# Layer norm of a convolution mixer: small products pinned in TensorE's order, its steps with priority, ACT's tables loaded early, the first four output chunks together, a tap every 2.9 blocks

## The chip, the core and the metric

The kernel runs on one core of a Trainium2 chip. The time is the device time in microseconds from launch to end; lower is better. PE is TensorE (matmuls; PEld its weight loads), DVE is VectorE, ACT is ScalarE, POOL is GpSimd, SP is SyncE, whose queue issues the weight transfers.

## The reference

Two layers at 256 tokens of 2048 features in float32. Layer 0 mixes with a convolution branch and a pooling branch, layer 1 with a short convolution; each is followed by a gated feed-forward block of 5632. The change lies in layer 0's mixer:

```python
def conv_pool_mixer(x, norm_g, w_in, conv_w, conv_b, ln_g, ln_b, w_pool, pool_scale, w_out):
    h = rms_norm(x, norm_g)
    u = h @ w_in
    a_val = u[..., :D_CONV]
    a_gate = u[..., D_CONV:2 * D_CONV]
    b_in = u[..., 2 * D_CONV:]
    a = a_val * jax.nn.sigmoid(a_gate)
    a = causal_depthwise_conv(a, conv_w) + conv_b
    a = jax.nn.silu(layer_norm(a, ln_g, ln_b))
    p = multiscale_pool(b_in, w_pool, pool_scale)
    return jnp.concatenate([a, p], axis=-1) @ w_out
```

D_CONV is 1024 and the convolution has 31 taps. The layer norm runs over those 1024 features of a token.

## The kernel before

Features lie on the 128 partitions in chunks of 128, tokens (256) along the free axis. A weight block is 128 x 128. Weights arrive on SP's queue in an order fixed by `_layout`, and are split on the core in pieces of eight blocks into a rounded part `hi` (a cast on ACT, L125) and a rest `lo` (a subtraction on DVE or, for the blocks in `POOL_SPLIT`, on POOL, L132). `hi` and `lo` have six buffers each, and a piece is prepared four pieces ahead. In the mixer a block's product is three matmuls (L177 to L179): `hi` by the rounded half of the input, `hi` by its rest, `lo` by the rounded half. The accumulators `acc` have five banks; the small totals `st` share one bank.

The mixer runs in this order: input projections of the convolution and pooling chunks (`M0_ORDER`); the small products of the pooling branch, which write `xs` anew through `split` (L210 on ACT, L211 on DVE); the pool half of the output projection, `project(xs, POOL_CHUNKS)`, 16 output chunks of eight blocks, each added to the residual `h` (L324); then the convolution half, `project(cat, range(NA), norm)`, 16 chunks of eight blocks.

Beside this the convolution runs on DVE and ACT. `tick` is called after each block's product and takes steps from queues by the costs in `PACE`: a tap of two chunks every 3.2 blocks (`tap`, L397 on ACT, L400 to L404 on DVE), into the tile `side`. Behind the third of the four pairs the mean of six chunks is taken (`ln_mean`, L431) and subtracted (`ln_center`). Behind the fourth pair (`convolved`, L410) come `ln_shift` (the rest of the mean, L457 and L450), `ln_squares` (the variance, L450), `ln_rstd` (`spread_over`: root, reciprocal and one refining step, then a diagonal `diag` that the product L274 spreads over all partitions) and `ln_out` (scale, Silu, split into `cat`: L481 to L486). `drain` empties the queues ahead of the convolution half. ACT needs a table for Sqrt, one for Sigmoid and one for Silu, and loads it where the function first occurs after another.

What is written in this order is then placed by a scheduler with priorities, which fixes each engine's order of instructions; every engine issues in that order.

Of the kernel before, what the change touches and what calls it, by code (L numbers as in the profile page):

```python
# [11 lines left out]
F32 = mybir.dt.float32  # L12
# [5 lines left out]
P = 128  # L18
# [66 lines left out]

WARM = 9

POOL_SPLIT = range(96, 24 * NC + 16 + 7 * NC + 8)
# [3 lines left out]
PACE = {"dve": 3.2, "ln": 3.0, "wait": 1.0, "now": 0.0}  # L92
# [3 lines left out]
def block_kernel(ctx: ExitStack, tc: tile.TileContext, xtok: bass.AP, vec: bass.AP, wall: bass.AP, out: bass.AP):  # L96
# [55 lines left out]
    queues = {name: deque() for name in ("dve", "ln", "wait")}  # L152
# [19 lines left out]
    def product(acc, hi, lo, x, first, last, wide):  # L172
        if wide:
            nc.tensor.matmul(acc, hi, x, start=first, stop=False, skip_group_check=True)  # L174
            nc.tensor.matmul(acc[:, T:], lo, x[:, :T], start=False, stop=last, skip_group_check=True)  # L175
        else:
            nc.tensor.matmul(acc[:, :T], hi, x[:, :T], start=first, stop=False)  # L177
            nc.tensor.matmul(acc[:, :T], hi, x[:, T:], start=False, stop=False)  # L178
            nc.tensor.matmul(acc[:, :T], lo, x[:, :T], start=False, stop=last)  # L179
# [43 lines left out]
    nc.gpsimd.memset(ones, 1.0)  # L223

# [14 lines left out]
    def rsqrt_of(*totals, scale, halves=False, st=None):  # L239
# [9 lines left out]
        return spread_over(small, st, scale, halves)  # L249

    def spread_over(small, st, scale, halves=False):
# [3 lines left out]
        nc.scalar.activation(root, st, AF.Sqrt, scale=scale, bias=eps)  # L255
        nc.vector.tensor_scalar(out=var, in0=st, scalar1=scale, scalar2=EPS, op0=ALU.mult, op1=ALU.add)
# [7 lines left out]
        spread = [ps.tile([P, P], F32, name="half", tag="acc") for _ in range(2)] if halves else None  # L264
        for j in range(2):
            nc.vector.tensor_tensor(out=diag[:, j * P : (j + 1) * P], in0=identity, in1=e[:, j : j + 1].broadcast_to([P, P]), op=ALU.mult)
            if halves:
                nc.tensor.matmul(spread[j], ones, diag[:, j * P : (j + 1) * P], start=True, stop=True)
        return spread or over_features(diag)

    def over_features(x):

        st = ps_st.tile([P, T], F32, name="st", tag="st")
        nc.tensor.matmul(st, ones, x, start=True, stop=True)  # L274
        return st

    class Norm:
# [30 lines left out]
        def rstd(self, sums=None):  # L308
            st = rsqrt_of(*self.sums, scale=1.0 / D, st=sums)
# [4 lines left out]
    def project(src, ks, norm=None, wide=False, narrow_end=False):  # L314

        for n in range(NC):
            if narrow_end and n == NC - 1:
                wide = False
            (acc,) = matmul_chunks(src, ks, wide=wide)
# [5 lines left out]
            if norm is not None:  # L325
                norm.add(n)

# [47 lines left out]
    with tc.tile_pool(name="m0", bufs=1) as m0, tc.tile_pool(name="ps_side", bufs=2, space=PSUM) as ps_side:  # L375
# [30 lines left out]
        def convolved(c):  # L406

            side = sides.pop(c)
            if c == NA - 2:
                nc.vector.tensor_tensor(out=conv[:, c:, :], in0=side, in1=pair(state["mean"]), op=ALU.subtract)  # L410
# [287 lines left out]
```

## Time and profile before

| what | us |
|---|---|
| median of 3 runs | 2121.29 |
| lowest and highest run | 2116.45, 2122.05 |
| the profiled execution, its own time | 2117.58 |
| its span from the first to the last instruction | 2115.5 |
| DVE busy, ACT busy, POOL busy | 1390.2, 1060.8, 200.5 |

The mixer of layer 0 takes the first 250 us or so: its input projections run to about 148 us, the pooling products to 157, the pool half of the output projection to 205, the convolution half from 213. In the views a row is a group of instructions: start, busy time, engine, line, operation, the tile written and the tiles read; a bracket tells how long the engine was idle before and what ended that.

### The profile page before, as it was taken

What the parts mean: (1) busy time and instruction counts of PE and PEld (TensorE: products, weight loads), DVE (VectorE), ACT (ScalarE), POOL (GpSimd) and SP (SyncE); (2) the same over time, 40 slices, a digit from 0 to 9 for tenths busy, and PEclk for the clock granted to TensorE, in tenths of its full rate; (3) what the DMA queues carried; (4) which work ended last, traced back from release to release, by engine and by line L of the source; (5) the groups of instructions that cost most, each with busy time, mean ns of one, the idle gap of its engine ahead of it and who ended that gap; (6) DMA issues with size and microseconds to landing.
All of it is one profiled execution on the core that took longest, in us unless ns stands there. A gap on an engine that the chain in (4) does not pass through costs nothing.

```text
span 2115.5 us, 31587 instructions
## 1 busy us (share of the span) xinstructions
PE 2091.5 (99%) x12568; PEld 1859.4 (88%) x12568; DVE 1390.2 (66%) x1984; ACT 1060.8 (50%) x1575; POOL 200.5 (9%) x180
## 2 busy tenths in 40 slices
PE   9998999999999999999999999999999999999997
PEld 9998988888888888888888888888888888888886
DVE  6998766666556666666777777766665556666554
ACT  7776654444444444455444445554444444444453
POOL 3984200000000000011000001100000000000011
PEclk9999999999999999999999999999999999999999
DMA  8555455555555455555555555555555555555551
GB/s 327 197 178 181 140 182 196 186 193 187 192 185 193 179 188 191 181 189 188 179 198 182 197 183 196 180 189 190 192 186 194 185 189 189 180 192 186 182 194 63
DMA packets 57428, 395.53 MB, mean 187 GB/s; under 512 B 6464, under 2 KB 7488, under 8 KB 10560
## 3 DMA queue, kind: packets, MB, share of 16 engines
q1 hardware_dynamic: 56992, 393.25, 52.0%
q8 instruction: 98, 1.61, 0.3%
q14 instruction: 50, 0.41, 0.1%
q10 hardware_dynamic: 288, 0.26, 0.0%
HBM read 391.39 MB, written 2.10 MB: 186 GB/s over the span
## 4 chain that ended last, share of the span: by engine, by line
PE 98%; DVE 1%; ACT 0%; DMA 0%; SPq 0%; issue 0%; DVEq 0%; ACTq 0%
PE acc L174 57%; PE acc L175 29%; PE acc L177 4%; PE acc L179 4%; PE acc L178 4%; DMA w<-in_wall 0%; DVE h L606 0%; ACT hi L125 0%; PE st L248 0%; PE st L274 0%; DVE lo L132 0%; ACT conv L483 0%; DVE conv L438 0%; SPq L115 0%; PE st L450 0%
## 5 line engine op out<-in xcount | busy, mean ns | idle before, releaser
L132 DVE TENSOR_TENSOR lo<-w,hi 128x1024 fp32r<-128x1024 f32 (+1 forms) x691 | 845.9, 1224 | 652.1 <-ACT hi L125 646.3
L125 ACT CAST hi<-w 128x1024 fp32r<-128x1024 f32 (+1 forms) x740 | 774.9, 1048 | 981.1 <-PE acc L174 632.1
L174 PE MATMUL acc<-xs,hi 128*128 128x512 f32 x3584 | 1253.9, 395 | 0.0
L175 PE MATMUL acc<-xs,lo 128*128 128x256 f32 x3584 | 1004.7, 280 | 0.0
L174 PEld LDWEIGHTS acc<-xs,hi 128*128 128x128 f32 x3584 | 671.6, 187 | 155.9
L175 PEld LDWEIGHTS acc<-xs,lo 128*128 128x128 f32 x3584 | 677.2, 189 | 0.1
L174 PE MATMUL acc<-y,hi 128*128 128x512 f32 x1386 | 486.7, 395 | 0.0
L175 PE MATMUL acc<-y,lo 128*128 128x256 f32 x1386 | 389.0, 281 | 0.0
L174 PEld LDWEIGHTS acc<-y,hi 128*128 128x128 f32 x1386 | 260.3, 188 | 61.2
L175 PEld LDWEIGHTS acc<-y,lo 128*128 128x128 f32 x1386 | 259.9, 188 | 0.4
L304 POOL TENSOR_TENSOR sumsq<-sumsq,sq 128x256 f32<-128x256 f32 x56 | 58.7, 1049 | 1613.4 <-ACT sq L302 1613.4
L177 PE MATMUL acc<-xs,hi 128*128 128x256 f32 x512 | 144.0, 284 | 2.5 <-ACT hi L125 1.4
L178 PE MATMUL acc<-xs,hi 128*128 128x256 f32 x512 | 143.7, 283 | 0.0
L179 PE MATMUL acc<-xs,lo 128*128 128x256 f32 x512 | 140.9, 284 | 0.0
L132 POOL TENSOR_TENSOR lo<-w,hi 128x1024 fp32r<-128x1024 f32 x49 | 119.0, 2450 | 43.3 <-ACT hi L125 41.6
L177 PEld LDWEIGHTS acc<-xs,hi 128*128 128x128 f32 x512 | 98.2, 192 | 3.6 <-ACT hi L125 2.2
L178 PEld LDWEIGHTS acc<-xs,hi 128*128 128x128 f32 x512 | 98.4, 192 | 0.0
L179 PEld LDWEIGHTS acc<-xs,lo 128*128 128x128 f32 x512 | 96.5, 192 | 0.3 <-DVE lo L132 0.3
L174 PE MATMUL acc<-z,hi 128*128 128x512 f32 x256 | 89.4, 394 | 0.0
L199 ACT COPY cross<-acc 128x256 f32<-128x256 f32 x224 | 81.7, 365 | 0.0
L175 PE MATMUL acc<-z,lo 128*128 128x256 f32 x256 | 71.6, 280 | 0.0
L397 ACT ACTIVATE prod<-a_in,v 128x256 f32<-128x256 f32 x120 | 54.2, 503 | 12.7 <-DVE side L404 12.3
(132 smaller groups left out, 1201.9 us busy)
## 6 DMA issues: line engine op xcount, KB each, us to landing
w<-in_wall SPq DMA_DIRECT2D x365, 1024.0 KB, 4.8
w<-in_wall SPq DMA_DIRECT2D x7, 512.0 KB, 6.9
rows<-in_xtok SPq DMA_DIRECT2D x4, 512.0 KB, 7.7
h<-in_wall SPq DMA_DIRECT2D x7, 256.0 KB, 6.7
out<-h SPq DMA_DIRECT2D x3, 512.0 KB, 2.7
v<-in_vec SPq DMA_DIRECT2D x1, 260.0 KB, 6.6
h<-in_wall ACTq DMA_DIRECT2D x2, 128.0 KB, 2.3
w<-in_wall SPq DMA_DIRECT2D x1, 256.0 KB, 5.1
```

The source lines that it names most:

```text
L125: nc.scalar.copy(hi[:, : n * P], w)
L132: engine.tensor_tensor(out=lo[:, : n * P], in0=w, in1=hi[:, : n * P], op=ALU.subtract)
L174: nc.tensor.matmul(acc, hi, x, start=first, stop=False, skip_group_check=True)
L175: nc.tensor.matmul(acc[:, T:], lo, x[:, :T], start=False, stop=last, skip_group_check=True)
L177: nc.tensor.matmul(acc[:, :T], hi, x[:, :T], start=first, stop=False)
L178: nc.tensor.matmul(acc[:, :T], hi, x[:, T:], start=False, stop=False)
L179: nc.tensor.matmul(acc[:, :T], lo, x[:, :T], start=False, stop=last)
L199: nc.scalar.copy(t, acc[:, T:])
L304: nc.gpsimd.tensor_tensor(out=self.sums[0], in0=self.sums[0], in1=sq, op=ALU.add)
L397: nc.scalar.activation(prods[c, k + 1][:, j, :], a_in[:, c + j, k + 1 : k + 1 + T], AF.Copy, scale=col("conv_w_e", (c + j) * CW + k + 1))
```

## The change

Seven things change. `ln_shift` and `ln_squares` become `ln_sums`: the wide product and the products by token read `conv` and the squares directly, with the share 1/1024 in a constant `shares`, so that DVE's additions and ACT's scaling ahead of them go, and two wide and ten narrow products stand where one and six stood. They are tied behind the matmul last written when the step is taken, and the next 64 blocks' products behind them; the spread product likewise (`pin`). The layer norm's steps get a high priority. The Sqrt table is loaded behind the last sigmoid, the Silu table behind the root, the Sigmoid table behind the first root. A tap comes every 2.9 blocks, `ln_sums` 26 blocks behind the last and `ln_rstd` 14 behind that. `POOL_SPLIT` ends 24 blocks earlier. The convolution half computes its first four output chunks together, input by input, with the weights laid out so; `ln_out` begins with two single chunks.

```diff
-POOL_SPLIT = range(96, 24 * NC + 16 + 7 * NC + 8)
+POOL_SPLIT = range(96, 24 * NC + 16 + 6 * NC)
...
-PACE = {"dve": 3.2, "ln": 3.0, "wait": 1.0, "now": 0.0}
+PACE = {"dve": 2.9, "ln": 3.0, "sums": 26.0, "rstd": 14.0, "now": 0.0}
...
+    def product(*args):
+        if behind_it[1]:
+            behind_it[1] -= 1
+            with tc.issue_after(behind_it[0]):
+                multiply(*args)
+        else:
+            multiply(*args)
+
+    def pin(mm):
+
+        behind_it[:] = [mm.ins, 4 * NC]
...
         nc.scalar.activation(root, st, AF.Sqrt, scale=scale, bias=eps)
+        if then is not None:
+            nc.scalar.activation(warm, root[:, :1], then)
...
+        for n, acc in enumerate(matmul_chunks(src, ks, n=together) if together else ()):
+            added(n, acc)
+        for n in range(together, NC):
...
             if c == NA - 2:
-                nc.vector.tensor_tensor(out=conv[:, c:, :], in0=side, in1=pair(state["mean"]), op=ALU.subtract)
-                later("ln", "now", ln_shift)
-                later("ln", "ln", ln_squares, ln_rstd, *(partial(ln_out, c) for c in range(0, NA, 2)))
+                with tc.high_priority():
+                    nc.vector.tensor_tensor(out=conv[:, c:, :], in0=side, in1=pair(state["mean"]), op=ALU.subtract)
+                    state["sq"] = sq = m0.tile([P, 2, T], F32, name="pm", bufs=2)
+                    nc.scalar.activation(sq, conv[:, c:, :], AF.Square)
+                later("ln", "sums", ln_sums)
+                later("ln", "rstd", ln_rstd)
+                later("ln", "now", partial(ln_out, 0, 1), partial(ln_out, 1, 1), *(partial(ln_out, c, 2) for c in range(2, NA, 2)))
...
+        def ln_sums():
             state["st"] = st = ps_st.tile([P, 2 * T], F32, name="st", tag="st")
...
+            rest, sq = conv[:, NA - 2 :, :], state["sq"]
+            with tc.issue_after(latest[0]), tc.high_priority():
+                for j in range(2):
+                    nc.tensor.matmul(st[:, T:], shares, rest[:, j, :], start=j == 0, stop=j == 1)
+                per_token(st[:, 8:10], (rest[:, 0, :], rest[:, 1, :]), shares)
+                pin(per_token(st[:, :2], (total[:, 0, :], sq[:, 0, :], sq[:, 1, :]), shares))
+                shift = tmp.tile([P, 2], F32, name="var", bufs=1)
...
+                nc.vector.tensor_tensor(out=st[:, :2], in0=st[:, :2], in1=shift, op=ALU.subtract)
+                state["diag"] = diag_of(st, st[:, :2], 1.0, AF.Silu)
...
         def ln_rstd():
-            st = state["st"]
-            state["rstd"] = spread_over(st, st[:, :2], 1.0)
...
+            with tc.issue_after(latest[0]), tc.high_priority():
+                state["rstd"] = over_features(state["diag"], pinned=True)
...
+            if c == NA - 1:
+                nc.scalar.activation(warm, gate[:, :1], AF.Sqrt)
...
-        project(cat, range(NA), norm)
+        project(cat, range(NA), norm, together=TOGETHER)
...
-    put(o[:, :NA])
+    put(o[:TOGETHER, :NA].swapaxes(0, 1))
+    put(o[TOGETHER:, :NA])
```

Three places of the order. The first is PE's, in the pool half of the output projection, where the sums stand. Before, they stand inside the 15th output chunk (`acc_2739`), five blocks ahead of its end:

```order
L178 MATMUL acc_2739<-xs_78,hi_2554 128x256
L179 MATMUL acc_2739<-xs_78,lo_2555 128x256
L177 MATMUL acc_2739<-xs_78,hi_2554 128x256
L178 MATMUL acc_2739<-xs_78,hi_2554 128x256
L457 MATMUL st_2581<-rest_2579,ones_79 128x256
L450 MATMUL st_2581<-ones_79,rest_2579 128x1 x2
L450 MATMUL st_2581<-ones_79,total_196 128x1 x2
L450 MATMUL st_2581<-ones_79,pm_2592 128x1 x2
L179 MATMUL acc_2739<-xs_78,lo_2555 128x256
L177 MATMUL acc_2739<-xs_78,hi_2554 128x256
```

Now they stand inside the 13th (`acc_2627`), three blocks behind its start:

```order
L195 MATMUL acc_2627<-xs_78,hi_2489 128x256
L196 MATMUL acc_2627<-xs_78,lo_2490 128x256
L194 MATMUL acc_2627<-xs_78,hi_2489 128x256
L195 MATMUL acc_2627<-xs_78,hi_2489 128x256
L196 MATMUL acc_2627<-xs_78,lo_2490 128x256
L496 MATMUL st_2643<-conv_196,shares_81 128x256 x2
L488 MATMUL st_2643<-shares_81,conv_196 128x1 x4
L488 MATMUL st_2643<-shares_81,total_198 128x1 x2
L488 MATMUL st_2643<-shares_81,pm_2544 128x1 x4
L194 MATMUL acc_2627<-xs_78,hi_2489 128x256
L195 MATMUL acc_2627<-xs_78,hi_2489 128x256
```

They have moved ahead by 47 matmuls, and their operand is `conv` itself.

The second is DVE's order at the same place, where `conv` of the last two chunks is written (L410, now L444). Before, the row ahead of it is the residual add of the 12th output chunk (`acc_2614`):

```order
L402 SCALAR_TENSOR_TENSOR side_2096<-a_in_192,v_76,side_2096 128x256
L324 TENSOR_TENSOR h_77<-acc_2553,h_77 128x256
L402 SCALAR_TENSOR_TENSOR side_2096<-a_in_192,v_76,side_2096 128x256
L132 TENSOR_TENSOR lo_2669<-w_2558,hi_2668 128x1024
L404 TENSOR_TENSOR side_2096<-side_2096,prod_2563 128x512
L324 TENSOR_TENSOR h_77<-acc_2614,h_77 128x256
L410 TENSOR_TENSOR conv_194<-side_2096,mean_1984 128x512
L132 TENSOR_TENSOR lo_2711<-w_2558,hi_2710 128x1024
L454 TENSOR_TENSOR rest_2579<-conv_194 128x256
```

Now, with `acc_2597` the 12th chunk and `acc_2627` the 13th:

```order
L134 TENSOR_TENSOR lo_2629<-w_2570,hi_2628 128x1024
L435 SCALAR_TENSOR_TENSOR side_2096<-a_in_194,v_76,side_2096 128x256
L349 TENSOR_TENSOR h_77<-acc_2597,h_77 128x256
L435 SCALAR_TENSOR_TENSOR side_2096<-a_in_194,v_76,side_2096 128x256
L134 TENSOR_TENSOR lo_2694<-w_2570,hi_2693 128x1024
L437 TENSOR_TENSOR side_2096<-side_2096,prod_2501 128x512
L435 SCALAR_TENSOR_TENSOR side_2096<-a_in_194,v_76,side_2096 128x256 x2
L437 TENSOR_TENSOR side_2096<-side_2096,prod_2522 128x512
L444 TENSOR_TENSOR conv_196<-side_2096,mean_1922 128x512
L500 COPY var_2656<-st_2643 128x2
L501 TENSOR_TENSOR var_2656<-st_2643,var_2656 128x2
```

Between the 12th chunk's add and the subtraction now stand three taps (two of them with their pair add) and the split of the piece `hi_2693`, the sixth piece behind the one that the 12th chunk uses.

The third is ACT's order where the pooling products are cast into `xs`. Before:

```order
L490 ACTIVATE gate_2069<-gate_2069 128x256
L433 ACTIVATE mean_1984<-st_1981 128x256
L434 ACTIVATE st_1981<-st_1981 128x256
L210 ACTIVATE xs_78<-acc_2074,v_76 128x256
L397 ACTIVATE prod_2114<-a_in_192,v_76 128x256
L397 ACTIVATE prod_2151<-a_in_192,v_76 128x256
L397 ACTIVATE prod_2190<-a_in_192,v_76 128x256
L210 ACTIVATE xs_78<-acc_2089,v_76 128x256
L210 ACTIVATE xs_78<-acc_2101,v_76 128x256
```

Now:

```order
L524 ACTIVATE gate_2071<-gate_2071 128x256
L470 ACTIVATE mean_1922<-st_1919 128x256
L471 ACTIVATE st_1919<-st_1919 128x256
L529 ACT_TABLE_LOAD
L529 ACTIVATE warm_95<-gate_2071 128x1
L228 ACTIVATE xs_78<-acc_2077,v_76 128x256
L430 ACTIVATE prod_2111<-a_in_194,v_76 128x256
L430 ACTIVATE prod_2148<-a_in_194,v_76 128x256
L430 ACTIVATE prod_2187<-a_in_194,v_76 128x256
L228 ACTIVATE xs_78<-acc_2092,v_76 128x256
L228 ACTIVATE xs_78<-acc_2104,v_76 128x256
```

A table load and a one-element activation have come in ahead of the casts; the loads further on, inside the layer norm, stand elsewhere in turn.

More of the change, by code (lines that the diff above doesn't have):

```diff
@@ L248, in rsqrt_of, with diag_of @@
                 nc.tensor.matmul(st[:, j : j + 1], x[:, j * P : (j + 1) * P], ones[:, :1], start=i == j == 0, stop=i == len(totals) - 1, skip_group_check=True)
-        return spread_over(small, st, scale, halves)
-    def spread_over(small, st, scale, halves=False):
+        diag = diag_of(small, st, scale, then)
+        if not halves:
+            return over_features(diag)
+        spread = [ps.tile([P, P], F32, name="half", tag="acc") for _ in range(2)]
+        for j in range(2):
+            nc.tensor.matmul(spread[j], ones, diag[:, j * P : (j + 1) * P], start=True, stop=True)
+        return spread
+    def diag_of(small, st, scale, then=None):
         var, root, e = (small[:, 2 * i : 2 * i + 2] for i in range(1, 4))
@@ L312, in rstd, with project, added @@
             return r
[L314 to L319, printed above, removed]
+    def project(src, ks, norm=None, wide=False, narrow_end=False, together=0):
+        def added(n, acc):
             if wide:
@@ L446, in ln_center @@
                 nc.gpsimd.tensor_tensor(out=total[:, 0, :], in0=total[:, 0, :], in1=total[:, 1, :], op=ALU.add)
-        def per_token(dst, x, first, last):
-            for j in range(2):
-                nc.tensor.matmul(dst[:, j : j + 1], x[:, j * P : (j + 1) * P], ones[:, :1], start=first and j == 0, stop=last, skip_group_check=True)
-        def ln_shift():
-            rest = m0.tile([P, T], F32, name="rest", bufs=1)
-            nc.vector.tensor_tensor(out=rest, in0=conv[:, NA - 2, :], in1=conv[:, NA - 1, :], op=ALU.add)
-            state["st"] = st = ps_st.tile([P, 2 * T], F32, name="st", tag="st")
-            nc.scalar.activation(rest, rest, AF.Copy, scale=1.0 / DC)
-            nc.tensor.matmul(st[:, T:], ones, rest, start=True, stop=True)
-            per_token(st[:, 8:10], rest, True, True)
@@ L498, in block_kernel @@
         nc.vector.tensor_tensor(out=rowsq[:, :2], in0=rowsq[:, :2], in1=rowsq[:, 2:], op=ALU.add)
-        r = norm.rstd(rowsq[:, :2])
-        nc.scalar.activation(warm, r[:, :1], AF.Sigmoid)
+        with tc.high_priority():
+            r = norm.rstd(rowsq[:, :2], AF.Sigmoid)
         for c in range(2):
```

71 lines of the change are left out of this document (39 added, 32 removed).

## The prediction

> **What bounds the kernel now.** I read the page first, then the waits of TensorE (PE) in the first 400 us, then the timeline around each wait.
>
> ```profile
> span 2115.5 us, 31587 instructions
> PE 2091.5 (99%) x12568; PEld 1859.4 (88%) x12568; DVE 1390.2 (66%) x1984; ACT 1060.8 (50%) x1575; POOL 200.5 (9%) x180
> ```
>
> PE is busy for 99% of the span, so only its idle stretches and its slow stretches can be won. The waits of PE (engine, line, waited for: us in total, times, longest) lie in the stretch that the change touches:
>
> ```profile
> PE st L274 <- DVE diag L266: 3.5, 1, 3.5
> PE acc L177 <- ACT cat L485: 3.4, 1, 3.4
> PE acc L177 <- DVE xs L211: 1.4, 1, 1.4
> PE acc L177 <- DVE gate L331: 1.1, 1, 1.1
> ```
>
> The first two are the layer norm. Its PE timeline (start, us, engine, line, tiles):
>
> ```profile
> 198.31 0.59 PE L457 MATMUL st<-rest,ones 128*128 128x256 f32 x2
> 198.74 0.50 PE L450 MATMUL st<-ones,rest 128*128 128x1 f32 x4
> 200.00 0.36 PE L179 MATMUL acc<-xs,lo 128*128 128x256 f32 x1
> 204.75 0.28 PE L179 MATMUL acc<-xs,lo 128*128 128x256 f32 x1
> 208.52 1.19 PE L274 MATMUL st<-diag,ones 128*128 128x256 f32 x2 [3.49 <-DVE diag L266]
> 213.10 1.43 PE L177 MATMUL acc<-cat,hi 128*128 128x256 f32 x5 [3.39 <-ACT cat L485]
> ```
>
> and the windows around it (stretch, its length, busy time of PE, PEld, DVE, ACT, POOL, then the granted clock, DMA share, GB/s):
>
> ```profile
> 206.00:208.00 2.00, 0.00 (x0) 0.00 (x0) 1.81 (x5) 1.33 (x2) 0.00 (x0) 0.83 0.00 0
> 214.00:216.00 2.00, 2.00 (x11) 2.00 (x11) 0.43 (x1) 2.00 (x6) 0.00 (x0) 0.50 0.00 0
> 216.00:218.00 2.00, 2.00 (x13) 2.00 (x12) 1.47 (x3) 0.58 (x2) 0.00 (x0) 0.61 0.00 0
> 218.00:220.00 2.00, 2.00 (x19) 2.00 (x18) 0.00 (x0) 0.00 (x0) 0.00 (x0) 1.00 0.00 0
> ```
>
> PE has no projection matmul from 204.87 to 213.10, which is 8.2 us. The clock halves at about 207.3 (0.83 is one third of that window at 0.5) and returns at about 217.5 (0.61), so 4.4 us of matmuls run at half speed, a loss of 2.2. With the 1.7 us of small products (198.31 to 200.00), **the layer norm now costs PE 1.7 + 8.2 + 2.2 = 12.1 us** beyond its projections. That is all this part can give.
>
> **The change, part by part.** *Pinned sums.* They now stand nine matmuls behind the last one of the 12th output chunk, and what they read (`conv`, written at the new L444) stands on VectorE (DVE) behind the residual add of that same chunk. All durations are in the rows of before:
>
> ```profile
> 191.47 0.28 PE L179 MATMUL acc<-xs,lo 128*128 128x256 f32 x1
> 191.59 0.28 PE L177 MATMUL acc<-xs,hi 128*128 128x256 f32 x1
> 180.61 1.00 DVE L402 SCALAR_TENSOR_TENSOR side<-a_in,v,side 128x256 f32<-128x256 f32 x2
> 181.72 0.70 DVE L404 TENSOR_TENSOR side<-side,prod 128x512 f32<-128x512 f32 x1
> 187.05 1.23 DVE L132 TENSOR_TENSOR lo<-w,hi 128x1024 fp32r<-128x1024 f32 x1
> 188.19 0.48 DVE L402 SCALAR_TENSOR_TENSOR side<-a_in,v,side 128x256 f32<-128x256 f32 x1
> 191.06 0.69 DVE L404 TENSOR_TENSOR side<-side,prod 128x512 f32<-128x512 f32 x1
> 191.79 0.42 DVE L324 TENSOR_TENSOR h<-acc,h 128x256 f32<-128x256 f32 x1
> 192.13 0.68 DVE L410 TENSOR_TENSOR conv<-side,mean 128x512 f32<-128x512 f32 x1
> 191.73 1.05 ACT L125 CAST hi<-w 128x1024 fp32r<-128x1024 f32 x1 [1.84 <-PE acc L178]
> ```
>
> Call R the moment at which the add of chunk 12 may start: 191.79, 0.32 behind that chunk's last matmul (191.47). Matmuls issue every 0.12 (191.47, 191.59), so PE comes to the sums at 191.47 + 10 x 0.12 = R+0.88. On DVE there now stand: the add, to R+0.34 (192.13); one tap; a weight split, which cannot start before its cast, and that cast waits for chunk 12's buffer (the ACT row, released by PE), so it starts at R+1.02 and ends at R+2.16 (1.14, from 187.05 to 188.19); a pair add, 0.73 (191.06 to 191.79); two taps, 1.11 (180.61 to 181.72); a pair add, 0.73; L444, 0.68. That makes 1.02 + 1.14 + 0.73 + 1.11 + 0.73 + 0.68 = R+5.41. In before the same subtraction (L410) follows the add directly, and PE comes to its sums only at 198.31. **So PE stands still for 5.41 + 0.05 - 0.88 = 4.6 us**, and nothing behind the sums can pass them. The relation hangs on chunk 12's end, not on the clock time, so taps at 2.9 in place of 3.2 blocks don't help it: bounds 4.3 (DVE late nowhere, faster splits) and 4.9 (DVE 0.2 late already).
>
> The products themselves grow from one wide and six narrow to two and ten. Wide: 198.74 - 198.31 = 0.43; narrow: (200.00 - 198.74) / 6 = 0.21. So 0.86 + 2.10 = 2.96 us in place of 1.69.
>
> The clock: before, PE's 3.65 us without work ahead of 208.52 lost it; 4.4 us without work will too. I take the same 4.4 us at half speed after it, 2.2; bounds 0 (the 1.4 us wait for `xs` below lost none) and 4.4, twice that.
>
> The Trainium skill, "TensorE: Matmul & The Clock Gate", section "Part 1: The HAM clock gate", says that activity is judged in free-running windows of 3413 ns. The low stretch here, 207.3 to 217.5, is three such windows, so the trace agrees. By it the work at half speed would end within one window, an estimated loss of at most 1.7 in place of 2.2.
>
> *The chain behind the sums, and the first four output chunks.* Its rows, the first three from the same formula at the start of the kernel:
>
> ```profile
> 33.89 0.15 DVE L498 TENSOR_TENSOR rowsq<-rowsq 128x2 f32<-128x2 f32 x1
> 34.43 0.16 DVE L256 TENSOR_SCALAR st<-rowsq 128x2 f32<-128x2 f32 x1 [0.39 <-ACT st L255]
> 35.76 0.48 DVE L266 TENSOR_TENSOR diag<-v,st 128x128 f32<-128x128 f32 x2
> 200.76 2.48 DVE L473 TENSOR_TENSOR conv<-conv,st 128x512 f32<-128x512 f32 x4
> 210.47 2.07 ACT L483 ACTIVATE conv<-conv,v 128x256 f32<-128x256 f32 x4 [3.12 <-DVE conv L481]
> ```
>
> Let S be the end of the sums. Three tiny operations at 0.2 and the chain (33.89 to 36.24, 2.35) bring `diag` to S+3.0. In before ACT's table load stood inside this chain, and here it doesn't. The spread product stands 42 matmuls behind the sums, S+5.0, but it writes the only bank of `st`, which the four subtractions (2.48) still read until S+5.5: 0.5 us of waiting. It takes 0.43. Then DVE does an add, a split, an add (0.34 + 1.14 + 0.34 from S+5.5) and the first scaling at S+7.3; ACT two Silu at 0.52 and a narrow cast of about 0.4 to S+9.2. PE still has 45 matmuls, 5.4 us, and is at the first `cat` matmul at S+11.4. **The cover is enough, 2.2 us to spare**: the 8.2 us gap goes. Each later input is asked for 1.44 us after the last (four chunks of three matmuls) in place of 0.36, and arrives ahead; I leave 0.1 for the second halves from DVE. If the cover were gone, it would cost up to 2.
>
> Sum of the layer norm: 4.6 + 3.0 + 2.2 + 0.5 + 0.4 + 0.1 = 10.8, against 12.1: **1.3 us won**.
>
> *Tables early.* The Sqrt table now loads in the middle of another busy stretch:
>
> ```profile
> 151.57 0.47 ACT L210 ACTIVATE xs<-acc,v 128x256 fp32r<-128x256 f32 x1
> 158.71 0.53 ACT L210 ACTIVATE xs<-acc,v 128x256 fp32r<-128x256 f32 x1
> 159.38 0.48 DVE L211 SCALAR_TENSOR_TENSOR xs<-acc,v,xs 128x256 fp32r<-128x256 f32 x1
> 154.77 0.39 PE L177 MATMUL acc<-cat,hi 128*128 128x256 f32 x1 [1.37 <-DVE xs L211]
> 157.03 0.28 PE L177 MATMUL acc<-xs,hi 128*128 128x256 f32 x1
> 203.19 1.28 ACT L255 ACT_TABLE_LOAD   x1
> 204.48 0.24 ACT L255 ACTIVATE st<-st,eps 128x2 f32<-128x2 f32 x1
> ```
>
> ACT runs without a break from 151.57 to 159.24, and the eight casts of `xs` among it feed DVE's second halves, the last of which ends at 159.86. The first output chunk of the projection starts at 157.03 and needs that piece in its eighth block, 157.03 + 7 x 0.36 = 159.55: no slack. The load (1.28) and the one-element activation behind it (0.20) push all eight casts by 1.5; with 0.1 of waits in DVE's order the last piece comes 1.6 later, and so does PE. **1.6 us lost.** Bounds: -1.4 (the wait at 154.77 goes because its `xs` half now comes ahead of a tap on DVE, and ACT catches up) to 2.9 (twice the load and its activation).
>
> The row at 204.48 starts 0.01 us after the load at 203.19 has ended. The Trainium skill, "ScalarE: Activation LUTs", section "What ACT_TABLE_LOAD costs", counts some 1380 ns of draining on top of each load's 1283 ns. The trace shows the load but no drain behind it; by the page the term would be 3.0 in place of 1.6.
>
> *At nothing.* At the start the Sigmoid load moves up, but DVE's chain and the 1.1 us wait behind it stay. The new constant is filled while the first weights are still on their way. Three weight splits go from POOL to DVE, 3 x 1.14 us in chunks 8 to 10, where DVE has 0.34 + 0.40 + 1.14 + 0.73 = 2.6 of 2.88 us between two adds; without that slack they'd lengthen the 4.6. Behind the first four chunks DVE has four adds and four `xs` splits at once, but a chunk comes only every 2.88 us and there are five accumulators. The weights are as many bytes as before, only in another order, and from the feed-forward block on every engine does the same in the same order.
>
> **Sum.** -1.3 + 1.6 = +0.3 us. The profiled execution took 2117.58 (span 2115.5, 2.1 around it), which gives 2117.9. The median of the runs, 2121.29, lies 3.7 above it, so on its scale the forecast is 2121.6. About 0.3%, 6.4 us, is what a measurement of this kernel can tell from no change.
>
> **The rivals.** *The change does what it says*: operands are there when PE comes to the sums, as a tap every 2.9 blocks suggests (31 x 0.3 x 0.36 = 3.3 us earlier). Then the 4.6 and the 2.2 fall away, the layer norm costs 4.0 in place of 12.1, and with 1.6 lost it is 2121.3 - 8.1 + 1.6 = 2114.8; with the early load hidden too, 2113.2. For it: the diagonal and the first inputs have real cover. Against it: 5.41 against 0.88 follows from three dependences on chunk 12, none of which can be outrun.
>
> *Slower: the low clock outlasts the sums.* Twenty-odd weight loads with one column each may not count as work, so that the clock returns only 4.4 us after the projection has resumed. Then the 2.96 us of products take 5.9 (2.96 lost), and 4.4 us of matmuls at half speed behind them lose 2.2 more: 5.2 in place of the 2.2 taken. That is 3.0 more, 2124.6, and 2126 with the upper bound of the early load. It decides from the moment at which the wait is long enough to lower the clock, some 2.3 us of idling (205.03 to 207.3). Against it: in before the same products ran at full clock and left it up, but for 1.7 us only.
>
> *The early load is hidden*: ACT has waited enough by then that only the order of casts changes. Then 1.3 is won, 2120.0; against it stands that no idle time is shown on ACT there.
>
> **How the numbers follow.** Forecast 2121.6 with 0.63, its own range 2115.5 to 2125.3 (the layer norm 7.7 to 13.2 with its terms at their bounds and its cover in place, the early load -1.4 to 2.9). The change doing what it says 0.14, most of it beyond 0.3%; the load hidden 0.10, within it; the low clock 0.13, a third of it beyond. From these: faster 0.13, within 0.81, slower 0.06. To hold 8 of 10 the range goes to 2114 at the fast end, halfway into that rival, and to 2126.5 at the other.
>
> **What would show it.** After's PE waits must name the new L496 waiting for DVE at L444 for 4 to 5 us, ten matmuls behind chunk 12, and a granted clock near 0.5 following it. No wait longer than 0.3 us for `cat`. The first chunk of the pool projection must wait 1 to 2 us for `xs` around 160. If L496 waits less than 1 us, or the clock stays at 1.0 there, the forecast is wrong on the fast side; if small products run at 0.4 us each for more than one window, the second rival is right.

## The result and the profile after

| what | us |
|---|---|
| before, median of 18 runs | 2121.19 (2115.28 to 2123.42) |
| after, median of 18 runs | 2129.14 (2120.74 to 2130.04) |
| after divided by before | 1.0036, 95% interval 1.0026 to 1.0047 |
| the profiled execution of after, its own time and its span | 2128.87, 2127.1 |

The change makes the kernel 8 us **slower**, by more than a measurement can miss; the forecast was 2121.6 with 2126.5 as the upper end. Single times lie in groups in both kernels: before near 2116 (6 of 18) and 2121.5, after near 2121.5 (4 of 18) and 2129. Any cause has to explain these groups too. Three executions that took far longer (one of before at 6057 us, two of b_start at 2933 and 5324 us) are left out of every median below.

The page of after:

```profile
span 2127.1 us, 31608 instructions
...
PE 2097.9 (99%) x12578; PEld 1866.2 (88%) x12578; DVE 1402.5 (66%) x1987; ACT 1060.2 (50%) x1577; POOL 191.2 (9%) x178
```

PE is busy 6.4 us more than before for the same projections and five small products more, so part of its work ran slower. Its waits from 20 to 300 us (engine, line, what it waited for: us in total, times, longest):

```profile
PE st L468 <- DVE total L453: 7.5, 1, 7.5
PE st L496 <- DVE conv L444: 4.4, 1, 4.4
PE st L300 <- ACT hi L127: 1.4, 1, 1.4
PE acc L194 <- DVE gate L364: 1.0, 1, 1.0
PE acc L194 <- DVE xs L229: 0.5, 1, 0.5
PE st L300 <- DVE conv L506: 0.3, 1, 0.3
```

The wait at L496 is the forecast one. The largest one is not: 7.5 us at the mean product (L468, formerly L431), a line that the change does not touch. Four moments of PE's timeline say where the 11.6 us between the two profiled spans came from:

| PE starts | before | after | later by | gained since the row above |
|---|---|---|---|---|
| the small products of the pooling branch | 147.83 | 150.93 | 3.1 | 3.1 |
| the pool half of the output projection | 157.03 | 167.97 | 10.9 | 7.8 |
| the first sums of the feed-forward block | 272.54 | 284.47 | 11.9 | 1.0 |
| end of the span | 2115.5 | 2127.1 | 11.6 | -0.3 |

So: the start 3.1, the mean product 7.8, the layer norm itself 1.0. Of the 7.8, PE's wait at the mean product is 6.8 longer than in before (7.5 beside 0.7); the granted clock fell during it as well, so that the first 3.8 us behind it (159.0 to 162.8) ran at half speed; and 0.9 us less was spent waiting for `xs`. (The profiled execution of before, 2117.58, was one of its quicker ones, 3.6 below the median; that is why 11.6 here are 8 in the medians.)

**The start.** The timeline of after at the first root mean square (start, us, engine, line, what was written and read):

```profile
34.82 1.28 ACT L284 ACT_TABLE_LOAD   x1
36.12 0.17 ACT L284 ACTIVATE warm<-st 128x1 f32<-128x1 f32 x1
...
36.32 0.16 DVE L285 TENSOR_SCALAR st<-rowsq 128x2 f32<-128x2 f32 x1 [1.88 <-ACT warm L284]
...
38.28 0.67 PE L300 MATMUL st<-diag,ones 128*128 128x256 f32 x2 [1.40 <-ACT hi L127]
```

and a window of it (stretch, length, busy PE, PEld, DVE, ACT, POOL, granted clock, DMA share, GB/s):

```profile
40.00:42.00 2.00, 2.00 (x9) 2.00 (x10) 2.00 (x7) 1.56 (x5) 2.00 (x2) 0.50 0.15 61
```

DVE's first operation of the formula waits for the early activation and so for the table load ahead of it, which was meant to stand beside the formula. The spread product comes at 38.28 in place of 36.66, and the longer stand lowers the granted clock to 0.50 behind it, where before had 1.00. (It does not fall in every execution: a_late36, below, has the same start and 1.00.)

**The mean product.** DVE's total (L453) is late since two operations of DVE lasted 7 and 9 us. The rows of DVE and POOL in after:

```profile
71.64 9.51 POOL L134 TENSOR_TENSOR lo<-w,hi 128x1024 fp32r<-128x1024 f32 x4
...
72.29 0.48 DVE L435 SCALAR_TENSOR_TENSOR side<-a_in,v,side 128x256 f32<-128x256 f32 x1
...
74.91 6.79 DVE L563 SCALAR_TENSOR_TENSOR cat<-pm,cat 128x512 fp32r<-128x512 f32 x1
...
108.98 9.49 POOL L134 TENSOR_TENSOR lo<-w,hi 128x1024 fp32r<-128x1024 f32 x4
110.37 8.65 DVE L563 SCALAR_TENSOR_TENSOR cat<-pm,cat 128x512 fp32r<-128x512 f32 x1
```

and in before:

```profile
73.71 1.22 DVE L527 SCALAR_TENSOR_TENSOR cat<-pm,cat 128x512 fp32r<-128x512 f32 x1
...
99.03 7.15 POOL L132 TENSOR_TENSOR lo<-w,hi 128x1024 fp32r<-128x1024 f32 x3
...
101.52 5.22 DVE L527 SCALAR_TENSOR_TENSOR cat<-pm,cat 128x512 fp32r<-128x512 f32 x1
```

Add start and length: the three long operations end at 81.70, 119.02 and 106.74; POOL's unbroken runs of weight splits ended at 81.15, 118.47 and 106.18. Each ends 0.55 us behind such a run, wherever in the run it arrived: here DVE is **held** until POOL pauses. A tap, with one of its inputs in PSUM (`side`), passes at 0.48 beside the same splits; L563 has both inputs (`pm` and `cat`) in SBUF. So has a weight split on DVE, and it is held too: 2.90 us at 133.93 in after, beside a POOL split that ended at 135.74, and 1.22 at 86.30, where POOL stood idle.

It is not held through the whole run every time. The row of before at 73.71 above ends at 74.93, 0.55 behind the first of three POOL splits in a row, and the second POOL split is the longer one instead:

```profile
71.98 2.40 POOL L132 TENSOR_TENSOR lo<-w,hi 128x1024 fp32r<-128x1024 f32 x1
74.35 2.86 POOL L132 TENSOR_TENSOR lo<-w,hi 128x1024 fp32r<-128x1024 f32 x1
```

Which of the two engines goes first between two splits differs between executions of one order of instructions (b_pace29, below); what decides it is not known.

**The layer norm.** The timeline of after behind chunk 12:

```profile
207.50 0.69 DVE L444 TENSOR_TENSOR conv<-side,mean 128x512 f32<-128x512 f32 x1
208.24 2.07 PE L496 MATMUL st<-conv,shares 128*128 128x256 f32 x4 [4.37 <-DVE conv L444]
...
212.53 1.84 PE L488 MATMUL st<-shares,pm 128*128 128x1 f32 x8
214.41 0.16 DVE L500 COPY var<-st 128x2 f32<-128x2 f32 x1 [6.22 <-PE st L488]
...
216.81 0.17 DVE L285 TENSOR_SCALAR st<-st 128x2 f32<-128x2 f32 x1 [1.85 <-ACT warm L284]
...
221.17 0.67 PE L300 MATMUL st<-diag,ones 128*128 128x256 f32 x2 [0.29 <-DVE conv L506]
...
227.07 0.64 PE L194 MATMUL acc<-cat,hi 128*128 128x256 f32 x4
```

and its windows (columns as above):

```profile
206.00:208.00 2.00, 0.00 (x0) 0.00 (x0) 1.90 (x4) 0.00 (x0) 0.00 (x0) 0.78 0.87 274
...
212.00:214.00 2.00, 2.00 (x11) 2.00 (x11) 0.00 (x0) 0.00 (x0) 0.00 (x0) 0.50 0.00 0
...
216.00:218.00 2.00, 2.00 (x14) 2.00 (x13) 1.02 (x6) 1.19 (x3) 0.00 (x0) 0.66 0.00 0
```

PE waits 4.4 us, in which the clock falls (0.78 in the first window), then spends 6.2 us on products that take 3.1 at full clock (a_split10, below, shows that). Then 2.9 us of the projection run at half speed, to 217.4, a loss of 1.5, and `cat` comes in time. That is 4.4 + 6.2 + 1.5 + 0.3 + 0.4 = 12.8 us, against the 12.1 of before.

### The profile page after: what moved, and what is told of

It reads as the page before. It is cut to its first block, busy times and chain, and to the rows that moved or that the text cites. A ratio compares the mean times of both kernels' runs of the same rounds, so it can differ in the third digit from the quotient of the medians.

```text
span 2127.1 us, 31608 instructions
## 1 busy us (share of the span) xinstructions
PE 2097.9 (99%) x12578; PEld 1866.2 (88%) x12578; DVE 1402.5 (66%) x1987; ACT 1060.2 (50%) x1577; POOL 191.2 (9%) x178
## 4 chain that ended last, share of the span: by engine, by line
PE 93%; DVE 5%; DMA 1%; ACT 1%; issue 0%; DVEq 0%; ACTq 0%
PE acc L191 57%; PE acc L192 29%; PE acc L194 2%; PE acc L195 2%; PE acc L196 2%; DVE side L435 1%; DMA w<-in_wall 1%; DVE side L437 1%; DVE cat L563 1%; DVE lo L134 0%; ACT hi L127 0%; ACT prod L430 0%; DVE h L642 0%; PE st L488 0%; PE st L268 0%
## 5 line engine op out<-in xcount | busy, mean ns | idle before, releaser
L134 POOL TENSOR_TENSOR lo<-w,hi 128x1024 fp32r<-128x1024 f32 x46 | 110.0, 2411 | 55.1 <-ACT hi L127 55.0
L430 ACT ACTIVATE prod<-a_in,v 128x256 f32<-128x256 f32 x120 | 54.4, 502 | 21.9 <-DVE side L437 21.1
```

What stands on the lines that cost most here:

```text
L134: engine.tensor_tensor(out=lo[:, : n * P], in0=w, in1=hi[:, : n * P], op=ALU.subtract)
L430: nc.scalar.activation(prods[c, k + 1][:, j, :], a_in[:, c + j, k + 1 : k + 1 + T], AF.Copy, scale=col("conv_w_e", (c + j) * CW + k + 1))
```

## The experiments

Medians are given beside the kernel before on the same chip in the same session (its median was 2120.7 to 2121.3, but 2116.8 in the last session), with the ratio and its 95% interval.

### Is DVE held by POOL? (a_port, b_port)

```diff
-            nc.scalar.activation(dst[:, :, :T], less, AF.Copy, scale=1.0 / w)
-            nc.vector.scalar_tensor_tensor(out=dst[:, :, T:], in0=less, scalar=1.0 / w, in1=dst[:, :, :T], ...)
+            nc.scalar.activation(less, less, AF.Copy, scale=1.0 / w)
+            nc.scalar.copy(dst[:, :, :T], less)
+            nc.gpsimd.tensor_tensor(out=dst[:, :, T:], in0=less, in1=dst[:, :, :T], op=ALU.subtract)
```

> The changed kernel with the low half of the four pooled groups of cat (VectorE, L563) computed on GpSimd from an input that ScalarE has scaled, so that VectorE has no operation with two SBUF inputs there. Theory 'held operation': L563 is held by GpSimd's unbroken run of weight splits (6.79 and 8.65 us for an operation that takes 0.55 alone), which makes the sum for the mean late. Then VectorE wins back some 15 us of standing between 70 and 150 us, the wait of TensorE at the mean product (7.5 us) falls under 1.5 us, the median falls by 6 to 8 us to about 2122, and the 18-run split into two groups some 8 us apart goes. Rival 'too much work': VectorE is late because taps come every 2.9 blocks and its work is what it is; then the edit takes only 4 x 0.55 = 2.2 us from it, the wait stays above 5 us and the median falls by at most 2.2 us.

> The kernel before with the same single edit (low halves of cat on GpSimd). 'Held operation': its runs lie in two groups as well (about 2116 and about 2122) because the operation is held in one of them; without it they fall together at 2114 to 2117, the median 4 to 6 us lower. 'Too much work': no change beyond 2 us, and the two groups stay.

a_port: 2118.98 (ratio 0.9997, 0.9988 to 1.0006), single times from 2117.5 to 2119.3. b_port: 2115.95 (0.9981, 0.9972 to 0.9990), from 2114.5 to 2117.2. The edit is worth 10 us in the changed kernel, more than the 6 to 8 expected, and 5 us in the one before, and **the groups are gone** in both. PE's waits in a_port:

```profile
PE st L496 <- DVE conv L444: 4.9, 1, 4.9
PE st L300 <- ACT hi L127: 1.4, 1, 1.4
PE acc L194 <- DVE gate L364: 1.0, 1, 1.0
PE acc L194 <- ACT hi L127: 0.3, 1, 0.3
```

The mean product is no longer among them. What remains between the two without holds is 3.0 us: the start and the layer norm. In the medians, then, 5 of the 8 us are holds.

### Do denser taps make the holds? (a_pace32raw, b_pace29)

```diff
-PACE = {"dve": 2.9, ...
+PACE = {"dve": 3.2, ...
```

for a_pace32raw, and the reverse in the kernel before for b_pace29.

> The changed kernel with one number of before put back: a tap every 3.2 blocks in place of 2.9 (the low halves of cat are on VectorE again). Theory 'held operation': TensorE's wait at the mean product follows the time that the four L563 are held, not the pace. Four traces so far give 10.6, 16.3, 20.4 and 21.9 us for the four L563 and waits of 0.7, 3.9, 7.5 and 7.9; this run falls on that line (wait = 0.68 x (sum - 10) within 1 us), whichever sum it draws. Rival 'denser taps overload VectorE': at 3.2 the wait is gone or 3 us and more smaller, off that line, and the median falls to 2121 to 2125.

> The kernel before with the new pace alone (2.9). 'Held operation': the pace moves the moment at which L527 reaches the lock, so the time may go either way, but the wait at L431 lies on the same line of held time (0.68 x (sum - 10), within 1 us). 'Denser taps overload VectorE': the wait at L431 rises to 4 us and more with L527 as short as before (10.6 us in all), and the median to 2125.

a_pace32raw: 2132.64 (1.0057, 1.0043 to 1.0071), holds of 20.4 us in all and a wait of 7.5 at the mean product, as in after: the pace has no part in them. Its extra 3.5 us come behind the mean: with later taps L444 stands behind the add of chunk 13, and the sums and `cat` are both waited for:

```profile
PE st L468 <- DVE total L453: 7.5, 1, 7.5
PE acc L194 <- ACT cat L519: 3.3, 1, 3.3
PE st L496 <- DVE conv L444: 2.4, 1, 2.4
```

b_pace29: 2120.22 (0.9997, 0.9987 to 1.0007). This run could not tell anything: the scheduler puts every engine's instructions in the same order at 2.9 as at 3.2, so it is the kernel before once more, with both of its groups. Its trace does show how far the holds are chance: the first two L527 last 5.96 and 1.53 us there, 1.22 and 5.22 in before.

Over all kernels with L563 on DVE, the wait at the mean product follows the time of its four executions:

| run | four L563 together, us | PE's wait at the mean, us |
|---|---|---|
| a_root (below) | 9.2 | none |
| before | 10.6 | 0.7 |
| b_pace29 | 11.7 | none |
| a_warm | 16.3 | 3.9 |
| a_startback | 17.0 | 4.6 |
| after | 20.4 | 7.5 |
| a_pace32raw | 20.4 | 7.5 |
| b_start | 20.6 | 7.7 |
| a_late36 | 21.9 | 7.9 |

### Which part made the holds longer? (a_startback, b_start)

Only the start changes an order ahead of the mean product. What it does to POOL's order, before and after (engine rows in program order):

```
25 L524 TENSOR_TENSOR pm<-sw,pm 128x512
26 L132 TENSOR_TENSOR lo<-w,hi 128x1024 x3
27 L521 TENSOR_TENSOR sw<-xp 128x2x262
...
26 L560 TENSOR_TENSOR pm<-sw,pm 128x512
27 L134 TENSOR_TENSOR lo<-w,hi 128x1024 x5
28 L557 TENSOR_TENSOR sw<-xp 128x2x262
```

Behind the first `pm`, from which L563 is computed, five splits stand in a row in place of three (four of them ran without a pause in after, the fifth had to wait for its cast). a_startback puts the start back in the changed kernel, b_start makes that edit alone in the kernel before:

```diff
-        with tc.high_priority():
-            r = norm.rstd(rowsq[:, :2], AF.Sigmoid)
+        r = norm.rstd(rowsq[:, :2])
+        nc.scalar.activation(warm, r[:, :1], AF.Sigmoid)
```

> The changed kernel with the start alone put back (no priority there, the Sigmoid table loaded by the one-element activation behind rstd as before). Its VectorE, ScalarE and GpSimd rows are then those of before up to the mean product, with the new layer norm behind it. Theory 'the early Sigmoid load makes the longer holds': the two groups of before come back, each higher by what the layer norm itself costs (0.7 to 1.0 us): median 2121.5 to 2122.5, single times around 2117 and 2122, none at 2129, and the four L563 hold VectorE for at most 16 us. Rival 'another part of the change': it stays at 2127 to 2129 with over 19 us of holds.

> The kernel before with the start of the change alone (Sigmoid load right behind the root, with priority). Theory: GpSimd then has five weight splits in a row behind the first pm (three before), the first two L527 are held 6 to 9 us each, and the mean product waits 7 to 8 us: median 2127.5 to 2129, the layer norm as in before. Rival 'another part of the change': within 2 us of before (2121), apart from 1 to 3 us at the start itself.

a_startback: 2122.14 (1.0005, 0.9996 to 1.0014), from 2118.3 to 2123.4. b_start: 2127.33 (1.0029, 1.0017 to 1.0041). The early Sigmoid load alone makes the kernel before 6.0 us slower, and without it the changed kernel is 0.8 above before. PE waits 7.7 us at the mean product in b_start, and DVE's timeline there has after's long rows:

```profile
74.41 7.00 DVE L529 SCALAR_TENSOR_TENSOR cat<-pm,cat 128x512 fp32r<-128x512 f32 x1
...
110.08 8.68 DVE L529 SCALAR_TENSOR_TENSOR cat<-pm,cat 128x512 fp32r<-128x512 f32 x1
```

### Why does the table load stand in the chain? (a_warm, a_root)

```diff
-            nc.scalar.activation(warm, root[:, :1], then)
+            nc.scalar.activation(warm, eps, then)
```

> The changed kernel, with the one-element activation that loads the next table reading a constant instead of the root. Theory 'tile-wide wait': VectorE's formula waits for that activation only because it reads the tile that VectorE writes next, so the table load stands in the chain after all; then VectorE's idle 1.88 us ahead of L285 at 36 us falls to about 0.4, the spread product at the start comes 1.4 to 1.6 us earlier, the half clock from 40 to 43 us goes (1.5 us more), the first product of a cat block comes about 3 us earlier, and the median falls by 1.5 (where VectorE's lateness then sets the mean product) to 3.4 us. Rival 'ScalarE's queue': the four weight casts and the load itself make it late, and the same wait stays: 0.

a_warm: 2124.05 (1.0015, 1.0005 to 1.0024). Faster, but not by the mechanism I meant: with nothing to wait for, the activation moved ahead of the root, and the Sqrt table was loaded again inside the formula:

```profile
33.60 1.28 ACT L282 ACT_TABLE_LOAD   x1
34.90 0.27 ACT L282 ACTIVATE st<-rowsq,eps 128x2 f32<-128x2 f32 x1
```

The clean test leaves the activation alone and gives the root a tile of its own:

```diff
+        root = tmp.tile([P, 2], F32, name="root", bufs=1)
-        var, root, e = (small[:, 2 * i : 2 * i + 2] for i in range(1, 4))
+        var, _, e = (small[:, 2 * i : 2 * i + 2] for i in range(1, 4))
```

> The changed kernel with the square root in a tile of its own, the early activation still reading it. (The run with a constant as its input did not test this: the activation went ahead of the root there, and the Sqrt and Sigmoid tables were loaded once more inside the chain.) Theory 'tile-wide wait': VectorE's first operation writes another part of the tile that the early activation reads, and waits for that reader. Then its idle time ahead of the formula falls from 1.88 to about 0.4 us at the start and from 1.85 to 0.4 behind the sums, the spread product at the start comes at 36.5 to 37 in place of 38.3, and GpSimd's order has two splits in a row behind the first pm in place of five, so that the holds fall below 17 us: median 2119 to 2123. Rival 'ScalarE serves one after the other': VectorE still waits for the load, 2127 to 2129.

a_root: 2107.42 (0.9953, 0.9938 to 0.9968). DVE and ACT in the formula at the start and behind the sums:

```profile
34.42 0.16 DVE L286 TENSOR_SCALAR st<-rowsq 128x2 f32<-128x2 f32 x1
...
34.81 0.17 DVE L287 RECIPROCAL inv<-root 128x2 f32<-128x2 f32 x1 [0.22 <-ACT root L283]
...
203.61 1.28 ACT L285 ACT_TABLE_LOAD   x1
203.63 0.17 DVE L286 TENSOR_SCALAR st<-st 128x2 f32<-128x2 f32 x1 [0.39 <-ACT root L283]
```

DVE now starts beside the load, PE's spread product comes at 36.65 as in before, two splits stand behind the first `pm`, and the holds are 9.2 us. So the wait came from the tile `small`, which the early activation read and DVE wrote, in other columns. (The edit also moves the root from `small`'s PSUM bank into SBUF; whether the wait goes by the tile or by the bank it doesn't tell.) The holds are not shorter by the two splits alone: behind the second `pm` five splits stand in a row in this trace, and L564 at 102.29 got in behind the first of them, after 1.32 us. The edit won 11 us more than the best that was expected: PE's first feed-forward sums come at 271.38 (after: 284.47), but the rest of the span is 1831.9 us long in place of 1842.6. That is taken up at the end.

### Can the sums be asked for later? (a_late36)

```diff
-PACE = {..., "sums": 26.0, ...
+PACE = {..., "sums": 36.0, ...
```

> The changed kernel with the pinned sums 10 blocks (3.6 us) later (26 to 36). Theory of the prediction: the sums wait 4.4 us only because they are asked for too early; then the wait at L496 falls to about 0.8 us, the clock stays at 1.0, the small products take 3.0 us in place of 6.2, and the wait for the first cat input rises to at most 0.5: 3.6 + 3.2 + 1.4 - 0.5, 7 to 8 us less between chunk 12 and the feed-forward block, median about 2122. Rival 'the wait moves': the inputs of cat come as late as the sums and TensorE stands there instead; then the gain is only what the clock gives, 3 to 4.6 us.

a_late36: 2133.30 (1.0059, 1.0046 to 1.0072), 4 us **slower**, missed by both theories. Its waits are nearly those of a_pace32raw: 2.4 at L496, 3.3 for `cat`. The scheduler had put one more add and one more weight split, both tied to PE's next chunk, ahead of L444, so DVE came later too; 2.4 us of waiting still lowered the clock; and the time that was missing behind the sums was then missing in front of `cat`.

### Can DVE be there earlier? (a_both, a_split10)

a_both is a_port with a_warm's edit, the base of the next runs; it keeps what was just said of a_warm, so the tables for Sqrt and Silu are loaded again in the layer norm. a_split10 adds

```diff
-POOL_SPLIT = range(96, 24 * NC + 16 + 6 * NC)
+POOL_SPLIT = range(96, 24 * NC + 16 + 10 * NC)
```

> The changed kernel with the low halves of cat on GpSimd and, besides, the table-loading activation reading a constant. If the two causes add up (the held operation and the table load inside the chain), the time lies 1.5 to 2.5 us below the first edit alone (2118.98): 2116.5 to 2117.5, with VectorE's wait ahead of L285 at the start at 0.4 in place of 1.88 us and the spread product about 1.4 us earlier. If ScalarE's casts were the cause of the late start, it stays at 2119. The wait at L496 stays 4 to 5 us in both cases, with the small products at half clock (about 6.2 us).

> As the run with both edits, and the weight splits up to the tenth chunk of that projection and beyond (96 to 24 NC + 16 + 10 NC) on GpSimd, so that VectorE has only taps and adds there and L444 comes before the 12th add. Theory of the prediction: the sums wait only because VectorE reaches L444 late, and all that follows (small products at half speed, 6.2 in place of 3.0 us; some 2.5 us of matmuls at half speed behind them) hangs on that wait. Then the wait at L496 is under 0.3 us, the clock stays at 1.0, and some 9 us go (4.9 + 3.2 + 1.2): 2107 to 2109. Rival 'GpSimd too slow': a split takes 2.41 us there in place of 1.14, TensorE waits for lo instead, and the time stays within 3 us of the run with both edits. Rival 'narrow products lower the clock by themselves': the wait goes, but the clock falls behind them all the same, 2111 to 2113.

a_both: 2119.14 (0.9996, 0.9987 to 1.0005), no gain over a_port. In its trace the pooling products start 0.9 us earlier, but the clock stays at 0.50 behind the sums until 210.0, in place of 207.8 in a_port: what the early activation gave is lost there. a_split10: 2110.07 (0.9956, 0.9941 to 0.9970), 9.1 us less. The sums there:

```profile
189.65 0.69 DVE L444 TENSOR_TENSOR conv<-side,mean 128x512 f32<-128x512 f32 x1
...
191.75 1.02 PE L496 MATMUL st<-conv,shares 128*128 128x256 f32 x4
...
193.87 1.03 PE L488 MATMUL st<-shares,pm 128*128 128x1 f32 x8
```

and a window of them:

```profile
192.00:194.00 2.00, 2.00 (x18) 1.92 (x16) 0.00 (x0) 0.00 (x0) 1.98 (x1) 1.00 0.34 139
```

With these splits off DVE, L444 stands before the 12th add and ends 1.4 us before PE asks. No wait, clock 1.00, products from 191.75 to 194.90, 3.1 us. So the wait and the doubled products were one cause, DVE's place, worth 9 us with the half clock behind them. (The change had moved the end of `POOL_SPLIT` the other way, from 7.5 chunks to 6; whether 7.5 would do was not tried.) The clock is not settled by this one trace: see a_rstd19 below.

### Parts that cost or bring nothing (a_nosqrt, a_tog0, a_nopin)

```diff
-            if c == NA - 1:
-                nc.scalar.activation(warm, gate[:, :1], AF.Sqrt)
```

> As the run with both edits, without the early load of the Sqrt table at L529 (it then loads at the formula behind the sums). By the step of the prediction, the early load delays the last xs piece by 1.6 us and TensorE with it: the time falls by 1.0 to 1.6 us, and the load behind the sums stays hidden (its 1.28 us end before the four subtractions do). Rival 'the order has room': the products on the last two xs pieces stand some 40 matmuls further back in TensorE's order, so the early load costs nothing: 0 (within 0.5 us).

a_nosqrt: 2119.55 (0.9997, 0.9988 to 1.0005), beside 2119.14: the load is free. In a_both two loads stood in that stretch, and PE waited 0.3 us for `xs` in all. In PE's order of before, 15 of the first output chunk's 24 products stand together, and the others, on the last pieces of `xs`, among the next chunks' up to 49 rows behind the first.

> As the run with both edits, without the four chunks together (0 in place of 4; the weights of the output projection back in their old order). ScalarE needs about 1.7 us for two inputs of cat, TensorE alone asks for two each 0.72 us: without the four chunks TensorE waits for cat 4 to 6 us in all, with a half clock behind it, 5 to 9 us slower: 2122 to 2126. Rival: the early tables and the order of steps are what covers the inputs, then within 1 us of the run with both edits.

a_tog0 (`TOGETHER = 0`): 2118.52 (0.9997, 0.9988 to 1.0007): the four chunks together bring nothing on this base, where the wait at L496 stands. PE's order there, written chunk by chunk, takes one to three products of four accumulators in turn as well; the scheduler does that by itself.

> As the run with both edits (2119.14), without the pins: the sums, the spread product and what follows stand where the scheduler puts them, all at the end of that projection. Theory: pinning as such brought nothing here, since the 4.9 us wait and the half clock of the pinned sums cost as much as the chain that stands open at the projection's end: sums 3.0, the open chain to the first input of cat 6 to 9 us, half clock 2: 2118 to 2122. Rival: the pins are worth the 8.2 us gap that the prediction counted, and the run is 6 us or more slower than 2119.14.

a_nopin (without `issue_after` and `pin`): 2119.70 (1.0002, 0.9993 to 1.0011), beside 2119.14. The sums slide to the end of the projection and the spread product then waits 6.6 us, `cat` 1.9. As long as DVE is late, the pins bring no more than they cost.

### A version that beats both (a_rstd19, a_split10_start, a_best17, a_best19)

> As the run with the splits on GpSimd (2110.07), with the spread product 5 blocks later (14 to 19). There L300 waited 1.7 us for the subtractions (L506) that read its bank, and TensorE came to cat 5.9 us behind the spread product, where 3.3 are needed. So the 1.7 us go and no wait for cat comes: 2108 to 2109. Rival: the wait moves to cat (a wait for L519 or L516 of 1 to 2 us): 2110.

> The fastest version so far (2110.07: low halves of cat on GpSimd, splits of that projection on GpSimd) with the start of before. With the holds gone the early load at the start has nothing left to win or to lose but the gap at the spread product, which was 0.7 us with the constant: within 1 us of 2110. If the early load still delays TensorE by its clock, it is 1 to 2 us faster: 2108 to 2109.

a_rstd19: 2110.80 (0.9958, 0.9944 to 0.9971): the wait for the subtractions went, 0.9 of it to `cat`, and nothing was won. The clock in its trace accounts for that. PE doesn't wait at the sums and is busy all through, and yet the granted clock is 0.50 from 195.9 to 199.3, right behind the narrow products, which costs some 1.7 us (half of 3.4):

```profile
196.00:198.00 2.00, 2.00 (x11) 2.00 (x11) 0.42 (x3) 1.54 (x3) 0.00 (x0) 0.50 0.75 303
```

The traces of a_best17 and a_best19 have the same low stretch, those of a_split10 and a_split10_start have none. So a_split10's second rival, that narrow products lower the clock by themselves, holds in three of these five traces, and the full clock of a_split10 was in part luck. The clock's changes in these traces lie on steps of 3.41 us; carried on, one such step holds 2.1 to 2.3 us of narrow products in the three, and at most 1.7 and 2.0 in the other two. That is an estimate from five traces, and no run tried it. a_split10_start: 2109.04 (0.9946, 0.9934 to 0.9958), 1.0 better.

> Low halves of cat and the splits of that projection on GpSimd, the start of before, the root in a tile of its own, the spread product 3 blocks later (14 to 17). Against 2109.04: the wait for the subtractions (1.7 us) shrinks by about 1.1 and the Silu table is loaded behind the root and not ahead of the first Silu, so no wait for cat comes in its place: 2107.5 to 2108.5. If the wait moves to cat: 2109.

> The same with 19 in place of 17: the 1.7 us go wholly if the inputs of cat still come in time (3.3 us are needed behind the spread product, 4.1 are there): 2107 to 2108. If the wait moves to cat: 2109 or more.

a_best17 (a_split10_start, the root in its own tile, `rstd` 17): **2097.36** (0.9906, 0.9893 to 0.9919). a_best19: 2097.65 (0.9905, 0.9891 to 0.9919). Some 11 us of that are again the shorter rest of the span (1831.5 in a_best17), which no theory had foreseen.

## Why the prediction was wrong

- **"At the start the Sigmoid load moves up, but DVE's chain and the 1.1 us wait behind it stay"**, under what costs nothing. This step failed, and it carries nearly all of the error. DVE's chain did not stay: it waits for the reader of its tile (1.88 us, a_root). The start lost 3.1 us in the profiled execution, with its half clock. And the moved start lengthened POOL's runs of splits, so that L563 was held 20.4 us in place of 10.6 and PE stood 7.5 us at the mean product (b_start: 6.0 us slower by this alone). With the start put back the time is 2122.14 (a_startback), 0.5 from the forecast; that this is so near is partly luck, since the layer norm cost 2.0 more and the early Sqrt load 1.6 less than forecast.
- The prediction did not look at the mean stage at all, since the change leaves its lines alone. The signs were there: L527 with 5.22 us beside 1.22, and single times of before at 2116.45 beside 2121.29 and 2122.05.
- **The wait of 4.6 us at L496**: 4.4 measured, 4.9 with nothing late in front of it (a_port), for the reason given: DVE's place behind chunk 12's add. a_split10 confirms it by taking that place away.
- **Products 2.96, half clock 2.2**: mis-sized. The products took 6.2 at half clock, with 1.5 behind them; together 2.5 more than forecast. This is the second rival's mechanism: the products did not bring the clock back, and it returned 2.9 us after the projection had resumed (the rival said 4.4). So the prediction's other estimate, that half speed ends within one step of 3.4 us of work, did not come out either: narrow products filled the step from 210.6 to 214.0 and the clock stayed low. And a_rstd19 shows that they can lower it with no wait ahead of them, which the prediction, going by the 1.7 us of sums in before, did not count.
- **Spread product 0.5 + 0.4, `cat` 0.1**: 0.3 + 0.4 and none. The cover was there, though the chain was 1.3 us longer by the wait for the Silu load. So the layer norm cost 12.8 in place of 10.8, and the 1.3 us won became about 1 us lost.
- **The 1.6 us lost by the early Sqrt load**: nothing (a_nosqrt); in after PE waits 0.5 us for `xs`, less than the 1.4 of before. That the chunk "needs that piece in its eighth block" overlooked that the scheduler had put those products behind others.
- **Taps at 2.9 don't help**: right for the mean. But the pace does decide behind which chunk's add L444 stands (a_pace32raw, 3.5 us).

## What to carry to other kernels

Before moving an operation that reads a tile which another engine writes, ask what that engine writes to it next: a harmless one-element read put a table load into DVE's chain. Where a row's longest execution is several times its shortest, find what stood on the neighbouring engine before its mean goes into any sum, and check whether single times come in groups. And since PE issues in order, an early request is paid twice when it waits long enough to lower the clock: here bringing the producer forward helped (a_split10), and moving the consumer back did not (a_late36).

## What was unexpected of the hardware

- DVE's operation with two SBUF inputs often did not get in between POOL's back-to-back splits: it was held through up to four of them (8.65 us for an operation that is done 0.55 us behind POOL's last one). In other executions it got in behind the first (1.22 us in before, 1.32 in a_root).
- While the clock was low, products of one column kept PE busy all through 210.1 to 214.2 us, and the clock came back only at about 217.4, after 3 us of wide matmuls; at full clock 2.3 us of the same products lowered it for 3.4 us in a_rstd19, a_best17 and a_best19, with PE busy throughout, and not in a_split10 and a_split10_start.
- The 11 us behind 272 us: with the root in its own tile, from 600 to 1000 us and from 1600 to 2000 PE issues 2301 or 2302 matmuls in each of the three kernels with that edit, and 2268 to 2277 in the other runs, with one exception below. At 840 us a block takes 0.347 us in place of 0.353, at a granted clock of 1.00 in both, though PE's order there is the same. All three ran on a chip of their own, but the kernel before ran on it too, at its usual 2115.4 to 2122.3. The new tile of eight bytes a partition moves the addresses of what is allocated behind it; that this is the cause was not tried. Against it stands a_late36, with no new tile and with after's order of PE in that block: it has the slow pitch from 300 to 650 us, where after has the fast one, and the fast one from 650 to 900 (2294 matmuls from 600 to 1000, 2276 from 1600 to 2000). So the pitch can shift without a new tile; what sets it stays open.
